# A decoder layer on one core: wide and narrow products in runs, a start with products of zeros, x loaded in quarters, and two token tiles on one weight unit

## The chip, the cores and the metric

The kernel runs on one core of one Trainium2 chip. The metric is the device time of one execution in microseconds. The kernel before took 653.57 us, the median of three runs (653.36 to 656.71).

## The reference

One post-norm decoder layer on x of 256 tokens by 1024 channels, in float32: a half-step SwiGLU, then attention and a gated short convolution side by side, then a second half-step SwiGLU, each with a residual and a layer norm.

```python
def swiglu(x, w_up, w_down):
    gate, up = jnp.split(x @ w_up, 2, axis=-1)
    return (jax.nn.silu(gate) * up) @ w_down

def hybrid_mixer(x, w_in, b_gate, conv_w, conv_b, w_proj_attn, w_proj_conv, w_out):
    z = x @ w_in                                  # q, k, v, h, g_b, g_c, gates
    y_attn = moba_attention(heads(q), heads(k), heads(v)) @ w_proj_attn
    y_conv = (g_b * short_conv(g_c * h, conv_w, conv_b)) @ w_proj_conv
    gate_attn, gate_conv = jnp.split(jax.nn.sigmoid(gates + b_gate), 2, axis=-1)
    return (gate_attn * y_attn + gate_conv * y_conv) @ w_out

x = layer_norm(ALPHA * x + 0.5 * swiglu(x, ffn1_w_up, ffn1_w_down), ln1_g, ln1_b)
x = layer_norm(ALPHA * x + hybrid_mixer(x, ...), ln2_g, ln2_b)
x = layer_norm(ALPHA * x + 0.5 * swiglu(x, ffn2_w_up, ffn2_w_down), ln3_g, ln3_b)
```

w_up is 1024 x 5632, w_down 2816 x 1024, w_in 1024 x 8192, and the three square matrices are 1024 x 1024. With 256 tokens there is one attention block, so attention is plain causal attention over 8 heads.

## The kernel before, in words

**Numbers in two parts.** Products run on float32r operands. Every operand a is split into a high part hi (a cast on ScalarE) and a low part lo = a - hi (a subtraction on VectorE), and a product is made of three passes: hi by hi, hi by lo, lo by hi. `split` (L175) does it for activations, `prep` (L809) for weights.

**Units.** The weights come in units of 128 x 2048 numbers (1 MB). SyncE loads a unit into one of three buffers `raw` (`load`, L799, the DMA at L804), ScalarE writes its high part (L814) and VectorE its low part (L817) into two of ten buffers `S`, in 2 chunks, or in 4 for the first two units of the layer. Such a buffer set is then used by TensorE until its last product.

**Three kinds of products.** `rows` (L268): the activations of one tile of 128 tokens are the stationary operand (the weights in the array), 512 columns of the unit move past them; 24 products of 512 columns for one tile and 512 outputs, over two units. `cols` (L290): 128 columns of the unit are stationary, the activations of both tiles move. For each of 8 slices k of the contraction there are two products. The wide one has u.hi stationary and 512 moving columns (the high parts of 256 tokens, then their low parts); the narrow one has u.lo stationary and 256 columns (high parts alone). The 16 products of such a group accumulate in one PSUM bank; `both` (L314) adds the two halves of the bank. `D` in `ffn` (L372): hidden activations stationary, w_down moving, 512 columns (256 at the very end).

In `cols` wide and narrow come in turns, but for the last slice, where the narrow one goes first:

```python
            two = [mm(... u.hi ..., k == 0, k == KT - 1, 512, u),
                   mm(... u.lo ..., False, False, 256, u)]
            ops += two if k < KT - 1 else two[::-1]
```

**Order.** The program is one list of products, `base`, written in the order of the layer. Transposes and attention are inserted at offsets in microseconds of a model clock (`put`, L112; L774 to L785). A last loop (L852) emits the list; before each product `advance` (L829) issues loads and casts ahead, as far as buffers and some constants allow. All engines then run their own instructions in that order and wait for each other by semaphores.

**The start.** SyncE loads tile 0 of x in two halves (`load_x(0)`, L446), the first unit in four quarters, tile 1 of x (L806), the second unit in four quarters. TensorE transposes x through PSUM, 128 columns at a time, four to a bank (`XT`, L245), and ScalarE and VectorE split the result into the tile `X`. Then `U_rows(0, 0)` and `U_rows(0, 1)` take the first 256 gate and 256 up columns of w_up by `rows`: all 24 products of tile 0 over both units, then all 24 of tile 1, with tile 1's transposes inserted. `U_cols` (L349) follows for the other hidden columns. Line numbers with L are those of the profile.

Of the kernel before, what the change touches and what calls it, by code (L numbers as in the profile page):

```python
# [9 lines left out]
F = mybir.dt.float32  # L10
R = mybir.dt.float32r
# [12 lines left out]
SCALE = 128 ** -0.5  # L24
NEG = -3.0e38

LEAD, LEAD0, LEAD1, PACE, DELAY, QUIET = 30.0, 0.1, 0.9, 2.2, 1.2, 4.0
OFF, AT0, AT1, AT2, HEAD = 5.0, 1.3, 10.5, 15.0, 7.5
AD1, AD2, AD3 = 2.0, 1.5, 1.0
S_BUFS, X_BUFS, RAW_BUFS, N_BUFS, T_BUFS, ACC_BUFS = 10, 3, 3, 9, 8, 8  # L30
# [35 lines left out]
def layer(ctx: ExitStack, tc: tile.TileContext, a: dict, out: bass.AP):  # L66
# [14 lines left out]
    state = {"dma": 0, "prep": 0, "chunk": 0, "t": -100.0, "hold": 0, "quiet": 0.0}  # L81


    ident = sb.tile([128, 128], F, name="ident")
    make_identity(nc, ident)
    mask = sb.tile([128, 128], F, name="mask")
# [3 lines left out]
    mhalf = sb.tile([128, 1], F, name="mhalf")  # L90
    nc.gpsimd.memset(mhalf, -0.5)
    cvec = sb.tile([128, 48], F, name="cvec")
    warm = sb.tile([128, 1], F, name="warm")
    nc.scalar.activation(warm, mhalf, AF.Silu)

# [4 lines left out]
    def mm(dst, lhsT, rhs, start, stop, cols, unit=None):  # L100
        return Op(lambda: nc.tensor.matmul(dst(), lhsT=lhsT(), rhs=rhs(), start=start, stop=stop), cols, unit)  # L101
# [10 lines left out]
    def put(at, dt, ops):  # L112

        ins.append((at, dt, ops))
# [6 lines left out]
    def new_unit(src, chunks=2):  # L121
        u = Unit(src, chunks)
        units.append(u)
        return u

    def row_units(w, c0, chunks=2, gap=None):

        res = []
        for kh in range(2):
            rows = w[kh * 512:(kh + 1) * 512, :]  # L130

            def src(raw, rows=rows):
# [24 lines left out]
    def transposes(src, n, evac):  # L157

        box = {}

        def go(i):
            if i == 0:
                box["t"] = ACC.get()
            nc.tensor.transpose(box["t"][:, i * 128:(i + 1) * 128], src(i), ident)  # L164

        ops = [Op(lambda i=i: go(i), 256) for i in range(n)]

        def fin():
            evac(box["t"])
            ACC.free()  # L170

        ops[-1].after.append(fin)
        return ops
# [94 lines left out]
    def rows(key, t, uns, epi):  # L268

        box, ops = {}, []  # L270
        for k in range(KT):
            u = uns[k // 4]
            ops += passes(lambda: box["b"], lambda s, k=k: st["xT", key][:, k, s, t, :],
                          lambda w, u=u, k=k: (u.hi, u.lo)[w][:, (k % 4) * 512:(k % 4 + 1) * 512],
                          k == 0, k == KT - 1, 512, u)
        f0 = ops[0].fn

        def first():
            box["b"] = ACC.get()
            f0()  # L280

        def fin():
            epi(box["b"])
            ACC.free()

        ops[0].fn = first
        ops[-1].after.append(fin)
        return add(ops)

    def cols(key, u, b, epi):  # L290

        box, ops = {}, []
        for k in range(KT):
            c = slice(k * 256 + b * 128, k * 256 + (b + 1) * 128)
            two = [mm(lambda: box["b"], lambda c=c: u.hi[:, c],
                      lambda k=k: st["xT", key][:, k].rearrange("p s t n -> p (s t n)"), k == 0, k == KT - 1, 512, u),
                   mm(lambda: box["b"][:, 0:256], lambda c=c: u.lo[:, c],
                      lambda k=k: st["xT", key][:, k, 0].rearrange("p t n -> p (t n)"), False, False, 256, u)]
            ops += two if k < KT - 1 else two[::-1]
        f0 = ops[0].fn  # L300

        def first():
            box["b"] = ACC.get()
            f0()

        def fin():
            epi(box["b"])
            ACC.free()

        ops[0].fn = first  # L310
        ops[-1].after.append(fin)
        return add(ops)
# [6 lines left out]
    def ffn(key, wu, wd, ln_i, by_rows, order, tail, after_ln):  # L319
# [9 lines left out]
        def U_rows(j, t):  # L329
            if j not in wun:  # L330
                wun[j] = row_units(wu, j * 256, 4 if key == "x" else 2, DFF)

            def epi(bank):
                sc = T.get()
                nc.scalar.activation(sc[:, 0:256], bank[:, 0:256], AF.Silu)
                nc.vector.tensor_tensor(sc[:, 256:512], sc[:, 0:256], bank[:, 256:512], op=OP.mult)
                st["h", j, t] = sc

            end = rows(key, t, wun[j], epi)
# [7 lines left out]
            put(end, OFF, transposes(lambda i: st["h", j, t][:, 256 + i * 128:256 + (i + 1) * 128], 2, evac))  # L347

        def U_cols(j):  # L349
            ug, uu = col_unit(wu, j * 256), col_unit(wu, DFF + j * 256)  # L350
# [63 lines left out]
                    op.after.insert(0, lambda: T.free(2))  # L414
            return add(ops)

        for j, t in order:
            U_rows(j, t)
        js = [j for j in range(by_rows, NJ)]
        done = 0  # L420
        for j in js:
# [12 lines left out]
        return e0, e1  # L434


    x2 = a["x"][0]
    for t in range(2):
        st["x", t] = N.get()

    def load_x(t):
        for h in range(2):
            c = slice(h * 512, (h + 1) * 512)
            nc.sync.dma_start(st["x", t][:, c], x2[t * 128:(t + 1) * 128, c])  # L444

    load_x(0)  # L446
    crow = sb.tile([48, 128], F, name="crow")

    def load_vectors():
# [4 lines left out]
    for half in range(2):  # L454
        add(XT("x", 0, lambda: st["x", 0], half))
    for half in range(2):
        put(len(base), 3.9 + 0.9 * half, XT("x", 1, lambda: st["x", 1], half))

    e0, e1 = ffn("x", a["ffn1_w_up"][0], a["ffn1_w_down"][0], 1, 1, ((0, 0), (0, 1)), 3, lambda t: ln_fin(t, 1))
    gb1_at = e0 - 150  # L460
    xt_after("m", 0, e0, 6.0, 6.9)
    xt_after("m", 1, e1, 8.2, 9.1)
# [336 lines left out]
    def load():  # L799
        while state["dma"] < len(order) and RAW.live < RAW_BUFS:  # L800
            u = order[state["dma"]]
            u.raw = RAW.get()
            for view, src in u.src(u.raw):
                nc.sync.dma_start(view, src)  # L804
            if state["dma"] == 0:
                load_x(1)  # L806
            state["dma"] += 1

    def prep(u, c):  # L809
# [77 lines left out]
```

## Time and profile before

| | |
|---|---|
| median of 3 runs | 653.57 us (653.36 to 656.71) |
| the profiled execution | 653.16 us, span of its instructions 651.3 us |
| TensorE products (PE) | 638.8 us busy, 98% of the span |
| weight loads into the array (PEld) | 547.5 us, 84% |
| VectorE (DVE), ScalarE (ACT), GpSimd (POOL) | 450.1 us, 357.1 us, 17.8 us |
| DMA | 121.18 MB, mean 186 GB/s |

How to read it: busy time of PE counts every product from its start to its modelled end, and products overlap, so neighbouring busy times add up to more than the span. The distance from one start to the next is what a product costs in a stream. A row of the timeline or of the chain merges products that follow each other with the same tiles, of whatever shape (the shape printed is one of them); its start is exact, so the difference of two rows' starts is the time of everything between. Idle time of the other engines costs nothing while TensorE goes on.

### The profile page before, as it was taken

The page shows a single profiled execution, that of the slowest core. Times are in us where ns is not written, and L with a number is a line of the kernel's source. Part 1 is how long each engine was busy: PE and PEld are TensorE (multiplying, and loading weights), DVE is VectorE, ACT ScalarE, POOL GpSimd, SP SyncE. Part 2 cuts the span into 40 slices and gives each one's busy share as a digit, 9 for nine tenths or more (in the row PEclk, how much of TensorE's full clock was granted, in tenths as well). Part 3 has the DMA queues.
Part 4 walks back from the last instruction along what each step waited for, and adds up shares of the span by engine and source line. Part 5 has one row for each costly group of instructions (what it writes and reads, how often), then busy time and mean ns, then how long its engine had stood idle before and what let it go on. Part 6 is the DMA issues. An engine that isn't in the chain of part 4 may idle for free.

```text
span 651.3 us, 8759 instructions
## 1 busy us (share of the span) xinstructions
PE 638.8 (98%) x3431; PEld 547.5 (84%) x3431; DVE 450.1 (69%) x707; ACT 357.1 (55%) x608; POOL 17.8 (3%) x26
## 2 busy tenths in 40 slices
PE   7999999999999999999999999999999999999995
PEld 5888888888888888888888888888888888888884
DVE  4786666666678576778659987886866666666636
ACT  4775555555534557667578655551556555555510
POOL 2000000000011000000000000001100000000002
PEclk9999999999999999999999999999999999999998
DMA  8856666557645572546647755572556755555301
GB/s 286 295 196 219 210 217 210 185 191 250 201 130 156 168 227 96 172 152 193 196 129 210 243 194 194 194 227 97 192 193 199 257 194 195 194 193 194 130 1 65
DMA packets 95853, 121.18 MB, mean 186 GB/s; under 512 B 2196, under 2 KB 84420, under 8 KB 95812
## 3 DMA queue, kind: packets, MB, share of 16 engines
q1 hardware_dynamic: 95812, 120.62, 56.9%
q8 instruction: 27, 0.44, 0.3%
q14 instruction: 14, 0.11, 0.0%
HBM read 119.56 MB, written 1.05 MB: 185 GB/s over the span
## 4 chain that ended last, share of the span: by engine, by line
PE 97%; DMA 1%; SPq 1%; POOL 0%; DVE 0%; issue 0%; ACT 0%; POOLq 0%
PE acc L101 96%; PE acc L164 1%; DMA raw<-in_ffn_w_up 1%; SPq L804 0%; SPq L444 0%; POOL rs L224 0%; POOL nmr L751 0%; DVE S L817 0%; ACT S L814 0%; POOLq L883 0%; POOL N L754 0%; DVE bn L214 0%; DVE N L212 0%; DVE mv L220 0%; PE acc L646 0%
## 5 line engine op out<-in xcount | busy, mean ns | idle before, releaser
L101 PE MATMUL acc<-X,S 128*128 128x512 f32 (+1 forms) x2368 | 424.5, 340 | 0.0
L101 PEld LDWEIGHTS acc<-X,S 128*128 128x128 f32 x2368 | 363.8, 189 | 53.5
L817 DVE TENSOR_TENSOR S<-raw,S 128x1024 fp32r<-128x1024 f32 (+1 forms) x224 | 268.5, 1205 | 43.4 <-ACT S L814 41.9
L814 ACT CAST S<-raw 128x1024 fp32r<-128x1024 f32 (+1 forms) x224 | 228.3, 1035 | 54.7 <-PE acc L101 49.3
L101 PE MATMUL acc<-S,T 128*128 128x512 f32 (+1 forms) x546 | 123.5, 383 | 0.0
L101 PEld LDWEIGHTS acc<-S,T 128*128 128x128 f32 x546 | 100.1, 188 | 19.4
L316 DVE TENSOR_TENSOR T<-T,acc 128x256 f32<-128x256 f32 x124 | 52.1, 420 | 86.4 <-ACT T L315 86.3
L315 ACT COPY T<-acc 128x256 f32<-128x256 f32 x124 | 46.1, 372 | 109.2 <-PE acc L101 108.2
L101 PE MATMUL acc<-S,X 128*128 128x512 f32 x336 | 82.8, 403 | 1.1 <-ACT S L814 0.9
L101 PEld LDWEIGHTS acc<-S,X 128*128 128x128 f32 x336 | 63.6, 193 | 16.0 <-ACT S L814 1.7
L177 ACT CAST X<-acc 128x512 fp32r<-128x512 f32 (+1 forms) x24 | 12.4, 516 | 27.5 <-PE acc L164 14.8
L187 ACT CAST T<-T 128x256 fp32r<-128x256 f32 x38 | 15.5, 408 | 19.3 <-DVE T L361 19.3
L178 DVE TENSOR_TENSOR X<-acc,X 128x512 fp32r<-128x512 f32 (+1 forms) x24 | 14.3, 598 | 14.7 <-ACT X L177 14.6
L355 ACT ACTIVATE T<-T 128x256 f32<-128x256 f32 x38 | 15.9, 418 | 11.2 <-DVE T L316 11.1
L212 DVE SCALAR_TENSOR_TENSOR N<-acc,N 128x512 f32<-128x512 f32 (+1 forms) x13 | 8.4, 644 | 15.8 <-PE acc L101 15.8
L224 POOL TENSOR_TENSOR rs<-ve,mhalf 128x1 f32<-128x1 f32 x6 | 5.8, 964 | 466.1 <-DVE ve L222 466.1
L182 DVE TENSOR_TENSOR T<-T,T 128x256 fp32r<-128x256 f32 x38 | 16.0, 420 | 1.9 <-ACT T L187 1.9
L361 DVE TENSOR_TENSOR T<-T 128x256 f32<-128x256 f32 x38 | 16.2, 425 | 1.3
L316 DVE TENSOR_TENSOR N<-N,acc 128x256 f32<-128x256 f32 x24 | 10.0, 418 | 9.1 <-ACT N L315 9.1
L315 ACT COPY N<-acc 128x256 f32<-128x256 f32 x24 | 8.9, 370 | 12.6 <-PE acc L101 12.3
L182 DVE TENSOR_TENSOR S<-T,S 128x256 fp32r<-128x256 f32 x16 | 6.8, 422 | 9.6 <-ACT S L187 9.6
L178 DVE TENSOR_TENSOR T<-acc,T 128x128 fp32r<-128x128 f32 (+1 forms) x20 | 7.9, 395 | 5.4 <-ACT T L177 5.4
(68 smaller groups left out, 199.7 us busy)
## 6 DMA issues: line engine op xcount, KB each, us to landing
raw<-in_ffn_w_up SPq DMA_DIRECT2D x38, 1024.0 KB, 5.1
raw<-in_w_in SPq DMA_DIRECT2D x32, 1024.0 KB, 5.5
raw<-in_ffn_w_down SPq DMA_DIRECT2D x22, 1024.0 KB, 4.9
raw<-in_w_proj_attn SPq DMA_DIRECT2D x4, 1024.0 KB, 5.1
raw<-in_w_proj_conv SPq DMA_DIRECT2D x4, 1024.0 KB, 5.0
raw<-in_w_out SPq DMA_DIRECT2D x4, 1024.0 KB, 4.9
raw<-in_ffn_w_up SPq DMA_DIRECT2D x8, 512.0 KB, 5.0
raw<-in_ffn_w_up SPq DMA_DIRECT2D x8, 256.0 KB, 5.8
```

Source lines behind the costliest of these rows:

```text
L101: return Op(lambda: nc.tensor.matmul(dst(), lhsT=lhsT(), rhs=rhs(), start=start, stop=stop), cols, unit)
L177: nc.scalar.copy(hi, src)
L178: nc.vector.tensor_tensor(lo, src, hi.bitcast(F), op=OP.subtract)
L182: nc.vector.tensor_tensor(lo, src, hi.bitcast(F), op=OP.subtract)
L187: nc.scalar.copy(hi, src)
L212: nc.vector.scalar_tensor_tensor(y[:, c], src, scale, st["ax", t][:, c], op0=OP.mult, op1=OP.add)
L315: nc.scalar.copy(dst, bank[:, 256:512])
L316: nc.vector.tensor_tensor(dst, dst, bank[:, 0:256], op=OP.add)
L355: defer(0.8, lambda: nc.scalar.activation(g[:, 0:256], g[:, 0:256], AF.Silu))
L361: nc.vector.tensor_tensor(g[:, 0:256], g[:, 0:256], g[:, 256:512], op=OP.mult)
L814: nc.scalar.copy(u.hi[:, s], u.raw[:, s])
L817: nc.vector.tensor_tensor(u.lo[:, s], u.raw[:, s], u.hi[:, s].bitcast(F), op=OP.subtract)
```

## The change

1. `cols` issues its sixteen products in runs: the first seven wide ones, the eight narrow ones, the last wide one.
2. The first two units are used by both tiles at once (`rows_both`, new): for each unit, the 12 products of tile 0 and then the 12 of tile 1, each tile in its own PSUM bank. Transposes of x stand between them.
3. x is loaded in four quarters of 128 x 512. The first goes out on ScalarE's queue ahead of its table load; the other three stand on SyncE's queue, one after the first two quarters of the first unit and two after its last (`early`).
4. Before the first transposes TensorE makes six products of 512 columns from a tile of zeros, `still`, which GpSimd fills first of all, and three more after the first four transposes (`idle`, new). Nothing reads their results.
5. The constant LEAD0 goes from 0.1 to -1.0, which delays the casts of weights in the list at the very start.

```diff
-LEAD, LEAD0, LEAD1, PACE, DELAY, QUIET = 30.0, 0.1, 0.9, 2.2, 1.2, 4.0
+LEAD, LEAD0, LEAD1, PACE, DELAY, QUIET = 30.0, -1.0, 0.9, 2.2, 1.2, 4.0
...
+    still = T.get(R)
+    nc.gpsimd.memset(still.bitcast(F), 0.0)
     ident = sb.tile([128, 128], F, name="ident")
...
+    load_x(0, 0, nc.scalar)
     warm = sb.tile([128, 1], F, name="warm")
     nc.scalar.activation(warm, mhalf, AF.Silu)
...
+    def idle(n):
+
+        def go():
+            b = ACC.get()
+            for i in range(n):
+                nc.tensor.matmul(b, lhsT=still[:, 0:128], rhs=still, start=i == 0, stop=i == n - 1)
+            ACC.free()
+
+        return [Op(go, 512 * n)]
...
+    def rows_both(key, uns, epis, between):
...
+        for half in range(2):
+            for t in range(2):
+                for k in range(half * 4, half * 4 + 4):
+                    u = uns[half]
+                    ops += passes(lambda t=t: box[t], lambda s, k=k, t=t: st["xT", key][:, k, s, t, :],
+                                  lambda w, u=u, k=k: (u.hi, u.lo)[w][:, (k % 4) * 512:(k % 4 + 1) * 512],
+                                  k == 0, k == KT - 1, 512, u)
...
+        for i in range(len(ops)):
+            for extra in between.get(i, []):
+                add(extra)
+            add([ops[i]])
...
     def cols(key, u, b, epi):
-        box, ops = {}, []
+        box, wide, narrow = {}, [], []
         for k in range(KT):
...
-            ops += two if k < KT - 1 else two[::-1]
+            wide.append(mm(lambda: box["b"], lambda c=c: u.hi[:, c],
...
+            narrow.append(mm(lambda: box["b"][:, 0:256], lambda c=c: u.lo[:, c],
...
+        ops = wide[:-1] + narrow + wide[-1:]
...
-        for j, t in order:
-            U_rows(j, t)
+        if key == "x":
+            U_both(0, order)
+        else:
+            for j, t in order:
+                U_rows(j, t)
...
-    load_x(0)
+    early = {1: [(1, 0)], 3: [(0, 1), (1, 1)]}
...
+    add(idle(6))
+    add(xts[0, 0])
+    add(idle(3))
+    base[-1].after.append(T.free)
+    e0, e1 = ffn("x", a["ffn1_w_up"][0], a["ffn1_w_down"][0], 1, 1,
+                 {6: [xts[1, 0]], 12: [xts[0, 1]], 18: [xts[1, 1]]}, 3, lambda t: ln_fin(t, 1))
...
-            for view, src in u.src(u.raw):
+            for i, (view, src) in enumerate(u.src(u.raw)):
                 nc.sync.dma_start(view, src)
-            if state["dma"] == 0:
-                load_x(1)
+                for t, h in early.get(i, []) if state["dma"] == 0 else []:
+                    load_x(t, h, nc.sync)
```

**On TensorE, one column group.** Before, the first group of `U_cols`; X are the activations, S_172 the unit's high part, S_173 its low part:

```order
L101 MATMUL acc_235<-X_102,S_172 128x512
L101 MATMUL acc_235<-X_102,S_173 128x256
L101 MATMUL acc_235<-X_102,S_172 128x512
L101 MATMUL acc_235<-X_102,S_173 128x256
L101 MATMUL acc_235<-X_102,S_172 128x512
L101 MATMUL acc_235<-X_102,S_173 128x256 x2
L101 MATMUL acc_235<-X_102,S_172 128x512
```

The same place in the changed kernel and the group behind it (S_195 and S_196 are the two parts, T_213 the hidden activations of tile 0):

```order
L112 MATMUL acc_163<-S_150,X_111 128x512
L112 MATMUL acc_235<-X_111,S_195 128x512 x7
L112 MATMUL acc_235<-X_111,S_196 128x256 x8
L185 MATMUL acc_255<-ident,T_213 128x128 x2
L112 MATMUL acc_235<-X_111,S_195 128x512
L112 MATMUL acc_271<-X_111,S_195 128x512 x7
L112 MATMUL acc_271<-X_111,S_196 128x256 x8
L112 MATMUL acc_271<-X_111,S_195 128x512
```

The last wide product of a group and the seven of the next stand in a row, so switches between the two widths go from fifteen a group to two. The transposes of tile 0's hidden activations, which before stood ahead of the first group, now stand inside it.

**On TensorE, the start.** The changed kernel's first rows (T_63 is the tile of zeros, N_78 and N_79 tiles 0 and 1 of x, S_118 and S_119 the first unit's two parts):

```order
L142 MATMUL acc_99<-T_63 128x512 x6
L185 MATMUL acc_106<-ident,N_78 128x128 x4
L142 MATMUL acc_114<-T_63 128x512 x3
L112 MATMUL acc_128<-S_118,X_111 128x512
L112 MATMUL acc_128<-S_119,X_111 128x512
L112 MATMUL acc_128<-S_118,X_111 128x512 x2
L112 MATMUL acc_128<-S_119,X_111 128x512
L112 MATMUL acc_128<-S_118,X_111 128x512
L185 MATMUL acc_137<-ident,N_79 128x128 x4
```

Before, the first rows were eight transposes of N_78, and then all 24 products of tile 0 over both units.

**On SyncE, the first loads.** Before (raw_83 and raw_90 are the first two units, raw_95 the third):

```order
L444 DMA N_78<-in_x 128x512 x2
L804 DMA raw_83<-in_ffn_w_up 128x2x256 x4
L444 DMA N_79<-in_x 128x512 x2
L804 DMA raw_90<-in_ffn_w_up 128x2x256 x4
L804 DMA raw_95<-in_ffn_w_up 128x8x256
```

In the changed kernel (raw_84, raw_92 and raw_97 in their places):

```order
L860 DMA raw_84<-in_ffn_w_up 128x2x256 x2
L101 DMA N_79<-in_x 128x512
L860 DMA raw_84<-in_ffn_w_up 128x2x256 x2
L101 DMA N_78<-in_x 128x512
L101 DMA N_79<-in_x 128x512
L860 DMA raw_92<-in_ffn_w_up 128x2x256 x4
L860 DMA raw_97<-in_ffn_w_up 128x8x256
```

Two quarters of weights now lead SyncE's queue, where two of x did; the quarter of x that is needed first is on ScalarE's queue.

## Rows read from the trace of the kernel before

**Rows 1.** The page: busy time of TensorE, and the chain that ended last, by engine.

```profile
PE 638.8 (98%) x3431; PEld 547.5 (84%) x3431; DVE 450.1 (69%) x707; ACT 357.1 (55%) x608; POOL 17.8 (3%) x26
...
PE 97%; DMA 1%; SPq 1%; POOL 0%; DVE 0%; issue 0%; ACT 0%; POOLq 0%
```

**Rows 2.** TensorE's two longest waits over the whole span: us in total, times, longest.

```profile
PE acc L164 <- DMA N<-in_x: 3.6, 1, 3.6
PE acc L101 <- ACT S L814: 0.9, 1, 0.9
```

**Rows 3.** Groups by line and shape, whole span: count, busy us, mean ns of one, idle.

```profile
L101 PE MATMUL acc<-X,S 128*128 128x512 f32 x1184 | 411.0, 398 | 0.0
...
L101 PE MATMUL acc<-X,S 128*128 128x256 f32 x1184 | 308.8, 281 | 0.0
...
L101 PEld LDWEIGHTS acc<-S,T 128*128 128x128 f32 x546 | 100.1, 188 | 19.4
...
L101 PE MATMUL acc<-S,T 128*128 128x256 f32 x36 | 4.5, 283 | 0.0
```

**Rows 4.** Timeline of TensorE, two stretches: start us, length us, what, count.

```profile
44.80 5.62 PE L101 MATMUL acc<-S,T 128*128 128x512 f32 x24
50.26 11.44 PE L101 MATMUL acc<-X,S 128*128 128x512 f32 x64
61.54 5.61 PE L101 MATMUL acc<-S,T 128*128 128x512 f32 x24
66.98 1.22 PE L101 MATMUL acc<-X,S 128*128 128x512 f32 x6
...
639.03 4.47 PE L101 MATMUL acc<-S,T 128*128 128x256 f32 x36
```

**Rows 5.** The chain that ended last, in order of time, from 475 us.

```profile
476.00 5.46 PE acc L101 x24
481.46 0.22 PE acc L164 x2
481.68 5.64 PE acc L101 x32
```

**Rows 6.** Timeline of the first 23 us, all engines, and of TensorE alone there.

```profile
0.27 0.10 POOL L876 MEMSET const-float32-1.0<- 128x1 f32 x1
...
0.71 0.21 POOL masks.py:197 MEMSET ident<- 128x128 f32 x1 [0.29 <-POOLq L876]
...
3.56 1.94 PE L164 MATMUL acc<-ident,N 128*128 128x128 f32 x8 [3.56 <-DMA N<-in_x]
...
4.68 0.59 ACT L177 CAST X<-acc 128x512 fp32r<-128x512 f32 x1 [2.47 <-PE acc L164]
...
6.35 0.69 DVE L817 TENSOR_TENSOR S<-raw,S 128x512 fp32r<-128x512 f32 x1 [0.36 <-ACT S L814]
...
6.37 6.03 PE L101 MATMUL acc<-S,X 128*128 128x512 f32 x13 [0.87 <-ACT S L814]
...
11.22 2.88 ACT L814 CAST S<-raw 128x512 fp32r<-128x512 f32 x4 [1.54 <-DMA raw<-in_ffn_w_up]
...
16.50 1.05 ACT L814 CAST S<-raw 128x1024 fp32r<-128x1024 f32 x1 [1.09 <-DMA raw<-in_ffn_w_up]
...
17.58 1.23 DVE L817 TENSOR_TENSOR S<-raw,S 128x1024 fp32r<-128x1024 f32 x1 [1.46 <-ACT S L814]
...
22.02 5.85 PE L101 MATMUL acc<-X,S 128*128 128x512 f32 x32
...
7.69 4.04 PE L101 MATMUL acc<-S,X 128*128 128x512 f32 x9
...
11.53 0.87 PE L101 MATMUL acc<-S,X 128*128 128x512 f32 x2
12.62 1.72 PE L101 MATMUL acc<-S,X 128*128 128x512 f32 x6 [0.22 <-DVE S L817]
```

**Rows 7.** Busy us of each engine in the first stretch, granted clock, DMA share, GB/s.

```profile
0.00:11.90 11.90, 7.47 (x20) 5.29 (x21) 3.90 (x7) 5.45 (x9) 3.28 (x11) 1.00 0.82 262
```

More of the change, by code (lines that the diff above doesn't have):

```diff
@@ L92, in layer, with load_x @@
     cvec = sb.tile([128, 48], F, name="cvec")
+    x2 = a["x"][0]
+    for t in range(2):
+        st["x", t] = N.get()
+    def load_x(t, h, engine):
+        c = slice(h * 512, (h + 1) * 512)
+        engine.dma_start(st["x", t][:, c], x2[t * 128:(t + 1) * 128, c])
+    load_x(0, 0, nc.scalar)
     warm = sb.tile([128, 1], F, name="warm")
@@ L288, in rows, with first, fin @@
         return add(ops)
+    def rows_both(key, uns, epis, between):
+        box, ops = {}, []
+        for half in range(2):
+            for t in range(2):
+                for k in range(half * 4, half * 4 + 4):
[3 more added lines that the diff above has]
+                                  k == 0, k == KT - 1, 512, u)
+        for t in range(2):
+            def first(t=t, f0=ops[12 * t].fn):
+                box[t] = ACC.get()
+                f0()
+            def fin(t=t):
+                epis[t](box[t])
+                ACC.free()
+            ops[12 * t].fn = first
+            ops[12 * t + 35].after.append(fin)
+        for i in range(len(ops)):
+            for extra in between.get(i, []):
+                add(extra)
+            add([ops[i]])
+        return len(base)
     def cols(key, u, b, epi):
-        box, ops = {}, []
+        box, wide, narrow = {}, [], []
         for k in range(KT):
             c = slice(k * 256 + b * 128, k * 256 + (b + 1) * 128)
[L295 to L298, printed above, removed]
-            ops += two if k < KT - 1 else two[::-1]
+            wide.append(mm(lambda: box["b"], lambda c=c: u.hi[:, c],
+                           lambda k=k: st["xT", key][:, k].rearrange("p s t n -> p (s t n)"),
+                           k == 0, k == KT - 1, 512, u))
+            narrow.append(mm(lambda: box["b"][:, 0:256], lambda c=c: u.lo[:, c],
+                             lambda k=k: st["xT", key][:, k, 0].rearrange("p t n -> p (t n)"), False, False, 256, u))
+        ops = wide[:-1] + narrow + wide[-1:]
         f0 = ops[0].fn
@@ L327, in hT_of, with U_epi, hT_put @@
             return st["hT", key, j, kk]
[L329 to L339, printed above, removed]
+        def U_epi(j, t, bank):
+            sc = T.get()
+            nc.scalar.activation(sc[:, 0:256], bank[:, 0:256], AF.Silu)
+            nc.vector.tensor_tensor(sc[:, 256:512], sc[:, 0:256], bank[:, 256:512], op=OP.mult)
+            st["h", j, t] = sc
+        def hT_put(j, t, at, dt):
             def evac(bank):
@@ L345, in evac, with U_rows, U_both @@
                     split(hT[:, 0], hT[:, 1], bank[:, kk * 128:(kk + 1) * 128])
-            put(end, OFF, transposes(lambda i: st["h", j, t][:, 256 + i * 128:256 + (i + 1) * 128], 2, evac))
+            put(at, dt, transposes(lambda i: st["h", j, t][:, 256 + i * 128:256 + (i + 1) * 128], 2, evac))
+        def U_rows(j, t):
+            if j not in wun:
+                wun[j] = row_units(wu, j * 256, 2, DFF)
+            hT_put(j, t, rows(key, t, wun[j], lambda bank: U_epi(j, t, bank)), OFF)
+        def U_both(j, between):
+            end = rows_both(key, row_units(wu, j * 256, 4, DFF),
+                            [lambda bank, t=t: U_epi(j, t, bank) for t in range(2)], between)
+            for t in range(2):
+                hT_put(j, t, end, OFF - 2.7 * (1 - t))
         def U_cols(j):
@@ L452, in load_vectors @@
         nc.sync.dma_start(crow[32:48], a["b_gate"][0].rearrange("(c p) -> c p", p=128))
[L454 to L459, printed above, removed]
+    xts = {(t, half): XT("x", t, lambda t=t: st["x", t], half) for t in range(2) for half in range(2)}
+    add(idle(6))
[4 more added lines that the diff above has]
+                 {6: [xts[1, 0]], 12: [xts[0, 1]], 18: [xts[1, 1]]}, 3, lambda t: ln_fin(t, 1))
     gb1_at = e0 - 150
```

7 lines of the change are left out of this document (removed).

## Prediction

> **What bounds the kernel now.** I read four views, in this order. The page's busy table and its chain of waits come first: TensorE is busy for 638.8 of 651.3 us, and 97% of the chain that ended last is products of TensorE [rows 1]. The reader should then ask whether TensorE ever waits. The list of TensorE's waits answers it: two waits of note, 4.5 us in all, and what they wait for (x, the first cast) belongs to the start [rows 2]. No transfer, no cast and no VectorE work holds TensorE up after that. What is left is what TensorE's own products cost one after another, and the first 22 us.
>
> The third view is the grouping of TensorE's work by shape: 1184 products of 512 columns (wide) and 1184 of 256 columns (narrow) come from the column helper, in 148 groups of 8 and 8 [rows 3]. A product's busy time there (398 and 281 ns) says little, because products overlap. What counts is the distance from one start to the next, so the fourth view is the timeline of TensorE, where the starts of neighbouring merged rows give the sums.
>
> - Wide in a run: 24 wide products take 50.26 - 44.80 = 5.46 us, and 66.98 - 61.54 = 5.44 us; 227 ns each [rows 4].
> - Wide and narrow in turns: 64 products, four column groups, take 61.54 - 50.26 = 11.28 us, which is 2.82 us a group [rows 4]. The chain gives the same in another place: 5.64 us for two groups, beside 5.46 us for 24 wide ones [rows 5].
> - Narrow in a run: 36 of them stretch over 4.47 us, of which the last one's own 283 ns is a tail: (4.47 - 0.28) / 35 = 120 ns each [rows 3, 4].
>
> So eight wide and eight narrow products would take 8 x 0.227 + 8 x 0.120 = 2.776 us if each kind ran as it does in runs, and they take 2.82 us in turns.
>
> **Runs in place of turns.** The change issues seven wide, eight narrow and one wide product; since the next group begins with wide ones, TensorE sees eight of a kind in a row. No instruction is added, and no operand differs. The gain is 2.820 - 2.776 = 44 ns a group, less what the two switches cost. A switch is not shown by itself; the nearest rows are the two stretches of 24 wide products, both entered from a column group: 5.46 and 5.44 us. One switch therefore costs 0.02 us more than another at most. I take 2 ns of it, near the cheap end, because the 120 ns of the narrow run already contain its entry. That makes 42 ns x 148 = **6.2 us**. The ends: with a full 0.02 us at the switch 24 ns x 148 = 3.6 us, and with 8 x 0.2267 (the 5.44 us) and 8 x 0.1197 and no price for a switch 48 ns x 148 = 7.1 us. All of it lies on the path, as TensorE waits for nothing there. The order also moves needs: the fifth wide product, which is the first to need the second half of a unit's high part, comes after 4 x 0.227 = 0.9 us instead of 1.4 us, and the low part is first needed after 1.6 us instead of 0.2 us. Casts that now precede TensorE without any wait cover a shift of half a microsecond.
>
> **The first 22 us.** Before, the first wide product starts at 6.37 us, and the next nine starts run from 7.69 to 11.53 us, 427 ns apart: that is 512 columns at 1.2 GHz. [...] (The column for the granted clock reads 1.00 for these first microseconds too [rows 7], which the distances contradict, so I read the level from the distances.) The 13 products from 6.37 to 12.62 us take 6.25 us instead of 13 x 0.227 = 2.95 us: 3.3 us are there to be had. The first column group starts at 22.02 us.
>
> The products of zeros give TensorE work earlier. The zeros come from a fill on GpSimd of 512 columns. Fills of 1 and of 128 columns take 0.10 and 0.21 us [rows 6], so some 0.5 us, from 0.7 to 1.25 us. Six products at 427 ns last from 1.3 to 3.9 us; x's quarter, issued at once on ScalarE's queue, should be there as before (3.56 us), so waiting for the zeros costs the first transpose 0.3 us. The cast of the transposes begins 1.12 us after the first of them (4.68 against 3.56), so at 5.0; 0.59 us for it and 0.62 us for the first quarter of weights give a first real product at about 6.3 us, **as before**. Nothing is won by an earlier start; what can be won is the clock. Before, it rose between 11.5 and 12.6 us, 5.2 to 6.2 us after the first wide product. From 1.3 us the same delay gives 6.5 to 7.5 us; I take 7.
>
> From there casts set the pace of the first quarters: VectorE's parts at 0.69 us each end near 6.95, 7.6, 8.3 and 9.0 us, so the tile's first 12 products end at about 9.9 us, the transposes woven between them included. Then, all at the higher clock: two sets of four transposes at 0.44 us, 12 products of the other tile, 24 products of the second unit, (12 + 24) x 0.227 + 0.88 = 9.05 us. The first column group starts at 18.95 us: 3.05 us earlier. One pair of transposes, 0.22 us [rows 5], which stood ahead of 22.02 us, now comes later. Net **2.8 us**. Are the weights there? ScalarE casts the four quarters of the second unit from 11.22 us on, waiting for the first; the last product needs the last one near 15.7 us, and they may only come earlier, as SyncE now issues weights first and passes one quarter of x to ScalarE's queue. The third unit is cast from 16.50 us, when it has landed: its halves are ready at 17.6 and 18.6 us, needed from 18.95 and 19.9 us; its low parts follow at 1.23 us a half, by 20.0 us, needed from 20.55 us. That fits, with half a microsecond to spare in the tightest place. The ends: if the clock rises no earlier than before, nothing is won; if the casts did not bind, 48 x 0.227 + 1.3 us from 6.3 us end at 18.5 us, which gives 3.3 us.
>
> Two tiles on a unit at once, seen alone, cost and save nothing in products. They halve the rate at which the first two units are wanted, which is why the higher clock can be used in spite of transfers. The ScalarE issue of 0.4 us stands before a table load that nobody waits for.
>
> **Sum.** 653.16 - 6.2 - 2.8 = 644.2 us against the profiled execution. That execution lies 0.4 us under the median of the three runs shown (653.57), so I forecast **644.6 us**. A measurement of this kernel can tell about 0.5%, some 3.3 us, from no change.
>
> **Rivals.**
> 1. The runs pay, the head does not: products of zeros leave the clock where it was, or transfers arrive so that 22.0 us stands. For it: no row here shows TensorE on zeros, and ScalarE waited 1.5 us for weights at 11.22 us. Against: the nine slow products were back to back, so it was the clock and not the data that bound them. 653.6 - 6.2 - 0.2 = 647.2 us.
> 2. The neighbours do not matter: a product's price depends on its columns alone, and the 2.82 us stay. Speaking for it: the runs of the trace take other weights and another moving operand than the column helper does. Against: both runs of wide products, with weights from different tiles, agree within 2 ns: those of [rows 4] hold hidden activations as weights, the 24 at 476.00 us of [rows 5] the layer's own. Then the head alone: 653.6 - 2.8 = 650.8 us. [...]
> 3. Slower: eight narrow products in a row run into their weight loads. A load takes 188 ns [rows 3], more than a narrow product; in turns every second product is wide and covers it. If loads cannot overlap each other, a narrow product in a run costs 188 ns, 8 x 68 ns x 148 = 81 us more: about 732 us. It decides as soon as a narrow product's distance passes 125 ns. Against it stand the 36 narrow products at 120 ns, each with a load of its own.
> 4. The change does not do what it says on the chip: wide and narrow stay mixed by a wait, for the second half of a unit, say. The orders above exclude it as far as the program goes; it would end near rival 2's time.
>
> **How the numbers follow.** Forecast 0.75; rival 1 0.13; rivals 2 and 4 0.09; rival 3 0.03. The forecast's own range is 653.6 less 3.6 to 7.1 and 0 to 3.3 us: 643.2 to 650, most of it below 647. Reaching up to rival 1, and down for a faster switch than I priced, 642.6 to 647.8 us leaves out the last 0.12 and the thin ends. Faster by over 0.5% (below 650.3): forecast and rival 1 with their ends, 0.88. Within: rivals 2 and 4, 0.09. Slower: rival 3, 0.03.
>
> **What would show it.** In the profile after, 64 products of column groups should take 11.1 us; more than 11.25 us proves the second step wrong. The first wide product of the layer should start near 6.3 us, the fifth and later at 227 ns once casts allow, and the first column group at about 19 us. If wide products still stand 427 ns apart at 9 us, the zeros failed. TensorE's waits should stay inside the first 10 us; a wait on a cast near 19 us would mean that the third unit came late.

## The result and the profile after

The changed kernel takes 649.80 us, the median of four runs (649.58 to 650.08), where the kernel before takes 653.47 us in the same comparison: a ratio of 0.9942, with a 95% interval of 0.9928 to 0.9957. It is faster by 0.6%, as the sign of the forecast said, but by 3.7 us and not by 9: 649.8 lies above the range of 642.6 to 647.8 us. The profiled execution took 650.08 us with a span of 648.1 us (before: 653.16 and 651.3), so the two traces differ by 3.2 us.

The page's busy line after the change, beside [rows 1]:

```profile
PE 638.3 (98%) x3440; PEld 548.9 (85%) x3440; DVE 449.8 (69%) x707; ACT 354.2 (55%) x608; POOL 18.5 (3%) x27
```

The list of TensorE's waits over the whole span, beside [rows 2] (us in total, times, longest):

```profile
PE acc L142 <- POOL T L85: 1.3, 1, 1.3
PE acc L112 <- ACT S L870: 0.3, 1, 0.3
PE acc L112 <- DVE S L873: 0.3, 1, 0.3
```

TensorE is still all of the kernel. The longest wait is now the one for the zeros, until 1.29 us, and behind the start there is none. So whatever is missing from the forecast sits in the starts of the products, not in a wait. First the head, in the timeline of TensorE (start us, length us, what, count, idle time before it):

```profile
1.29 2.93 PE L142 MATMUL acc<-T 128*128 128x512 f32 x6 [1.29 <-POOL T L85]
4.02 1.05 PE L185 MATMUL acc<-ident,N 128*128 128x128 f32 x4
4.73 1.21 PE L142 MATMUL acc<-T 128*128 128x512 f32 x3
6.27 0.50 PE L112 MATMUL acc<-S,X 128*128 128x512 f32 x1 [0.34 <-ACT S L870]
7.08 1.43 PE L112 MATMUL acc<-S,X 128*128 128x512 f32 x5 [0.31 <-DVE S L873]
8.35 0.60 PE L185 MATMUL acc<-ident,N 128*128 128x128 f32 x4
8.70 1.90 PE L112 MATMUL acc<-S,X 128*128 128x512 f32 x6
10.44 0.60 PE L185 MATMUL acc<-ident,N 128*128 128x128 f32 x4
...
12.61 7.08 PE L112 MATMUL acc<-S,X 128*128 128x512 f32 x30
19.53 2.70 PE L112 MATMUL acc<-X,S 128*128 128x512 f32 x15
```

The first real product starts at 6.27 us (before 6.37), and the first column group at 19.53 us instead of 22.02 [rows 6]. One pair of transposes, 0.22 us, now comes behind that point, so the head gained 2.3 us.

Then the stretch that answers to [rows 4], in the same columns:

```profile
42.29 5.75 PE L112 MATMUL acc<-S,T 128*128 128x512 f32 x24
47.88 11.31 PE L112 MATMUL acc<-X,S 128*128 128x512 f32 x64
59.03 5.75 PE L112 MATMUL acc<-S,T 128*128 128x512 f32 x24
64.62 5.73 PE L112 MATMUL acc<-X,S 128*128 128x512 f32 x32
```

Two things moved here, in opposite directions. Four column groups take 59.03 - 47.88 = 11.15 us instead of 11.28. Over all groups with nothing woven in, the mean of their starts went from 2.822 us (132 groups) to 2.794 us (131): 28 ns x 148 = 4.1 us gained. (By the order shown ahead of the prediction, a group before changes width fourteen times, not the fifteen named there; now it does so twice.) But the 24 wide products between the groups, those of `D`, take 47.88 - 42.29 = 5.59 us instead of 5.46 and 5.44: **233 ns each instead of 227**. The grouping by shape, first of the kernel before and then of the changed one, has the loss for the whole group (count, busy us, mean ns of one, idle):

```profile
L101 PE MATMUL acc<-S,T 128*128 128x512 f32 x510 | 119.2, 390 | 0.0
...
L112 PE MATMUL acc<-S,T 128*128 128x512 f32 x510 | 122.2, 395 | 0.0
```

There are 510 products, and their busy time is 3.0 us more than before. Taken from the starts, 5.8 ns x 510 = 3.0 us lost; over all neighbours within `D` the mean distance is 227.3 ns before and 233.3 ns after. The sum is -2.3 - 4.1 + 3.0 = -3.4 us, against -3.2 us of the spans.

Nothing in the change names `D`. The study therefore asked what made those 510 products dearer, and then what each of the two gains was made of.

### The profile page after: what moved, and what is told of

Same layout as the page of the kernel before. It is cut to its first block, busy times and chain, and to the rows that moved or that the text cites. A ratio compares the mean times of both kernels' runs of the same rounds, so it can differ in the third digit from the quotient of the medians.

```text
span 648.1 us, 8783 instructions
## 1 busy us (share of the span) xinstructions
PE 638.3 (98%) x3440; PEld 548.9 (85%) x3440; DVE 449.8 (69%) x707; ACT 354.2 (55%) x608; POOL 18.5 (3%) x27
## 4 chain that ended last, share of the span: by engine, by line
PE 98%; POOL 0%; DVE 0%; issue 0%; ACT 0%; POOLq 0%; DVEq 0%
PE acc L112 96%; PE acc L185 1%; PE acc L142 0%; POOL rs L245 0%; POOL nmr L807 0%; DVE S L873 0%; ACT X L198 0%; POOL T L85 0%; POOLq L939 0%; POOL N L810 0%; DVE bn L235 0%; DVE N L233 0%; DVE mv L241 0%; PE acc L702 0%; DVE ve L243 0%
## 5 line engine op out<-in xcount | busy, mean ns | idle before, releaser
L112 PE MATMUL acc<-S,T 128*128 128x512 f32 (+1 forms) x546 | 126.4, 387 | 0.0
L112 PE MATMUL acc<-S,X 128*128 128x512 f32 x336 | 80.3, 394 | 0.7 <-ACT S L870 0.3
L112 PEld LDWEIGHTS acc<-S,X 128*128 128x128 f32 x336 | 62.1, 188 | 14.2 <-DVE S L873 1.1
L416 ACT ACTIVATE T<-T 128x256 f32<-128x256 f32 x38 | 15.9, 418 | 11.6 <-DVE T L371 11.6
L198 ACT CAST T<-acc 128x128 fp32r<-128x128 f32 (+1 forms) x20 | 7.0, 350 | 7.8 <-DVE T L199 4.0
```

The costliest lines, as they stand in the source:

```text
L198: nc.scalar.copy(hi, src)
L416: defer(0.8, lambda: nc.scalar.activation(g[:, 0:256], g[:, 0:256], AF.Silu))
```

## The experiments

All of them compute the full layer. Each is compared with the kernel before, whose median lies between 653.3 and 653.6 us in all comparisons. Two theories for `D` stood at the start: the **place** of a buffer in SBUF (the tile of zeros is the first thing that pool T is asked for; pools are laid out in the order of first use, so T moves from byte 211104 of each partition, the top, to byte 16512, and raw, X and S move up by 16384; these places are worked out from the order and the sizes of the buffers in the kernels, as a trace shows no addresses), and the **entry** (a run of `D` now begins behind seven or eight narrow ones and a wide one).

**1. The runs alone.** The kernel before with the new order in `cols` and nothing else.

```diff
-            ops += two if k < KT - 1 else two[::-1]
...
+            wide.append(mm(... u.hi ..., 512, u))
+            narrow.append(mm(... u.lo ..., 256, u))
+        ops = wide[:-1] + narrow + wide[-1:]
```

> The kernel before with the new order of the column groups alone; T stays at the top of SBUF. Seen so far: in the changed kernel the products with hidden activations as weights (weights from T) stand 233 ns apart instead of 227, 510 of them, 3.1 us. Theory A (place): the tile of zeros is the first that asks for pool T, so T moves from the top of SBUF to its bottom, and loading weights from there slows the products. Then here they stay at 227 ns, the column groups take 2.793 us, and the time is 653.5 - 148 x 0.027 = 649.5 us. Theory B (entry): a run of wide products keeps the rhythm in which it is entered, and one wide product behind eight narrow ones starts the slow rhythm. Then they stand at 233 ns here too, and the time is 652.6 us.

Measured 649.62 us, ratio 0.9941 (0.9926 to 0.9956). TensorE's timeline:

```profile
44.62 5.62 PE L101 MATMUL acc<-S,T 128*128 128x512 f32 x24
50.08 11.31 PE L101 MATMUL acc<-X,S 128*128 128x512 f32 x64
```

`D` stays at 5.46 us for 24. The runs alone bring 4.0 us, no less than the whole change with its head: the order of the groups is not what hurt `D`.

**2. The place alone.** The kernel before, with pool T asked for first and given back at once. Not one instruction changes, only addresses.

```diff
+    T.get(R)
+    T.free()
     ident = sb.tile([128, 128], F, name="ident")
```

> The kernel before, in which nothing is changed but that one buffer of pool T is asked for and given back before any other tile, so that T lies at the bottom of SBUF as in the changed kernel. Theory A (place): products with weights from T at 233 ns, 653.5 + 3.1 = 656.6 us. Theory B (entry): 227 ns and 653.5 us.

Measured 656.00 us, ratio 1.0039 (1.0025 to 1.0054). TensorE's timeline:

```profile
44.61 5.75 PE L103 MATMUL acc<-S,T 128*128 128x512 f32 x24
50.20 11.43 PE L103 MATMUL acc<-X,S 128*128 128x512 f32 x64
61.47 5.75 PE L103 MATMUL acc<-S,T 128*128 128x512 f32 x24
```

50.20 - 44.61 = 5.59 us for 24, as in the changed kernel, while four column groups in turns take 11.27 us, as before. The place alone costs 2.4 us in medians, where theory A had 3.1 (the spans of the two traces, 653.9 and 651.3 us, lie 2.6 us apart).

**3. The change with the old places.** The zeros come from a buffer of pool N, whose place doesn't depend on it.

```diff
-    still = T.get(R)
+    still = N.get(R)[:, 0:512]
...
-    base[-1].after.append(T.free)
+    base[-1].after.append(N.free)
```

> The changed kernel with its zeros in a buffer of pool N instead of T, so that T, S, X and raw lie where they lay before. Theory A (place): products with weights from T at 227 ns, 649.8 - 3.1 = 646.7 us. Theory B (entry): 233 ns and 649.8 us.

Measured 647.43 us, ratio 0.9909 (0.9892 to 0.9925), 2.4 us below the change, where theory A had 3.1. TensorE's timeline:

```profile
42.09 5.62 PE L112 MATMUL acc<-S,T 128*128 128x512 f32 x24
47.55 11.32 PE L112 MATMUL acc<-X,S 128*128 128x512 f32 x64
58.70 5.62 PE L112 MATMUL acc<-S,T 128*128 128x512 f32 x24
```

`D` is back at 5.46 us, and the 64 products keep their 11.15 us. The following kernels start from this one where nothing else is said.

**4. The narrow run elsewhere.** The changed kernel, with one wide product ahead of the narrow run and seven behind it, so that `D` follows a run of wide ones.

```diff
-        ops = wide[:-1] + narrow + wide[-1:]
+        ops = wide[:1] + narrow + wide[1:]
```

> The changed kernel (T at the bottom) with the eight narrow products behind the first wide one, so that the last seven wide ones of a group lead into the products with weights from T. Theory A (place): these stay at 233 ns, the time stays within 0.3 us of 649.8. Theory B (entry): the run is in its fast rhythm when they come, 227 ns and 646.7 us. Under both a column group should stay near 2.793 us.

Measured 650.52 us, ratio 0.9955 (0.9940 to 0.9970). In its timeline `D` still takes 5.60 us:

```profile
42.30 5.75 PE L112 MATMUL acc<-S,T 128*128 128x512 f32 x24
47.90 11.34 PE L112 MATMUL acc<-X,S 128*128 128x512 f32 x64
59.08 5.75 PE L112 MATMUL acc<-S,T 128*128 128x512 f32 x24
```

The entry theory falls a second time. The median is 0.7 us above the change, and not within 0.3 us as theory A had it; the column groups take 59.08 - 47.90 = 11.18 us for four instead of 11.15, and why is open.

**5. No products of zeros.** Kernel 3 without its nine `idle` products, to see what they are worth; their buffer is given back at once.

```diff
-    add(idle(6))
     add(xts[0, 0])
-    add(idle(3))
...
+    N.free()
```

> As e3_old_places (647.4 us), without the nine products of zeros. Theory C (clock): the zeros are what raises TensorE's clock early; without them the wide products stand 427 ns apart until some 5.5 us after the first one, near 11.8 us, some 12 of them at 0.2 us more each, 2.4 us, and the time is 649.8 us, about that of e1_runs_only: quarters of x and both tiles on one unit bring nothing by themselves. Theory D (data): the order of loads and of tiles brings the gain; the time stays within 0.5 us of 647.4.

Measured 649.11 us, ratio 0.9934 (0.9917 to 0.9950): between the two theories, nearer to the clock's. TensorE's timeline:

```profile
3.53 1.08 PE L185 MATMUL acc<-ident,N 128*128 128x128 f32 x4 [3.53 <-DMA N<-in_x]
5.80 3.31 PE L112 MATMUL acc<-S,X 128*128 128x512 f32 x6 [1.19 <-ACT S L868]
8.91 1.06 PE L185 MATMUL acc<-ident,N 128*128 128x128 f32 x4
9.62 2.91 PE L112 MATMUL acc<-S,X 128*128 128x512 f32 x6
12.32 0.64 PE L185 MATMUL acc<-ident,N 128*128 128x128 f32 x4
12.72 1.66 PE L112 MATMUL acc<-S,X 128*128 128x512 f32 x6
14.21 0.60 PE L185 MATMUL acc<-ident,N 128*128 128x128 f32 x4
...
21.50 1.75 PE L112 MATMUL acc<-X,S 128*128 128x512 f32 x7
```

and of kernel 3, which has the zeros, at the same places:

```profile
4.73 1.63 PE L142 MATMUL acc<-N 128*128 128x512 f32 x3
6.27 2.27 PE L112 MATMUL acc<-S,X 128*128 128x512 f32 x6
8.38 0.60 PE L185 MATMUL acc<-ident,N 128*128 128x128 f32 x4
8.73 1.64 PE L112 MATMUL acc<-S,X 128*128 128x512 f32 x6
10.20 0.60 PE L185 MATMUL acc<-ident,N 128*128 128x128 f32 x4
10.56 1.64 PE L112 MATMUL acc<-S,X 128*128 128x512 f32 x6
12.04 0.60 PE L185 MATMUL acc<-ident,N 128*128 128x128 f32 x4
...
19.30 2.70 PE L112 MATMUL acc<-X,S 128*128 128x512 f32 x15
```

Without zeros the first product comes half a microsecond sooner, at 5.80 us, but the first three sets of six products take 8.91 - 5.80 = 3.11 us, 12.32 - 9.62 = 2.70 us and 14.21 - 12.72 = 1.49 us, where kernel 3 takes 2.11, 1.47 and 1.48 us. Six at the 427 ns of [rows 6] are 2.56 us, six at 227 ns 1.36 us: the long distances last until about 12.3 us here. The first column group starts at 21.50 us, with zeros at 19.30 us. The zeros are thus worth 2.2 us in starts and 1.7 us in medians. The rest of the start, 22.02 - 21.50 less 0.22 us of transposes, is 0.3 us. Quarters of x, two tiles on one unit and the new LEAD0 share it; no run separates them.

**6 and 7. What about the place?** Kernel 3 with T elsewhere. In 6 raw, X and T are asked for in that order behind the first small tiles, so that T lies below S, at byte 129184, and S at 145568, as in the change. In 7 T is asked for before raw, so that raw, X and S lie exactly as in the change, and T at 55456 below them all.

```diff
     crow = sb.tile([48, 128], F, name="crow")
+    for pool in (RAW, X, T):
+        pool.get()
+        pool.free()
```

```diff
     crow = sb.tile([48, 128], F, name="crow")
+    T.get()
+    T.free()
```

> As e3_old_places, with pool T between X and S (byte 129184 of a partition), which moves S up by 16384 bytes, to where the changed kernel has it; raw and X stay. Theory A1 (T at the bottom is what costs): weights from T at 227 ns, 647.4 us. Theory A2 (the new place of S, which moves past those weights, is what costs): 233 ns, 650.5 us.

> As e3_old_places, with pool T between N and raw (byte 55456): raw, X and S lie as in the changed kernel, T and N have changed places with each other. Theory A1: if any place far below S costs, 233 ns and 650.5 us; if only the lowest bytes do, 227 ns and 647.4 us. Theory A2 (place of S): 233 ns and 650.5 us. With e6 the three tell apart: 227 and 227 ns leaves the lowest bytes alone, 227 and 233 ns the distance below S, 233 and 233 ns the place of S.

Both measured 647.26 us, ratio 0.9908 (0.9894 to 0.9923 and 0.9893 to 0.9923), and both have `D` at 5.47 and 5.46 us. The timeline of 7:

```profile
42.05 5.62 PE L112 MATMUL acc<-S,T 128*128 128x512 f32 x24
47.51 11.32 PE L112 MATMUL acc<-X,S 128*128 128x512 f32 x64
```

Neither the place of S, nor T below S, nor a distance between them costs anything. Of the changed kernel's layout two things are left: that T is the lowest pool, and the exact byte. The buffers of X, S and T, and the slices of them that products take, lie at multiples of 512 bytes from their pool's start, so the pool's start counts. In the kernel before, in 3, 6 and 7, T and S both start 160 bytes past a multiple of 512. In the change and in 2, T starts at 128 and S at 160.

**8. Two groups woven.** Kernel 3 with both column groups of a unit at once: 14 wide, 16 narrow, 2 wide. It has half the switches.

```diff
-        ops = wide[:-1] + narrow + wide[-1:]
...
+        return add(wide[0][:-1] + wide[1][:-1] + narrow[0] + narrow[1] + wide[0][-1:] + wide[1][-1:])
```

> As e3_old_places, with the two column groups of a unit woven: sixteen wide products, then sixteen narrow ones, so half as many switches. In e3 a wide run needs five products behind a switch to come down to 227 ns (234, 235, 229, 232, 231), 26 ns in all over 5 x 227. If that is a price of the switch, a pair of groups takes 5.56 us instead of 5.587, 74 x 26 ns = 1.9 us less: 645.5 us. If the epilogues of two groups that now come together hold TensorE up, more than 647.4 us, with waits on ScalarE or VectorE.

Measured 646.35 us, ratio 0.9895 (0.9880 to 0.9910). TensorE's timeline:

```profile
47.59 11.28 PE L112 MATMUL acc<-X,S 128*128 128x512 f32 x64
58.71 5.61 PE L112 MATMUL acc<-S,T 128*128 128x512 f32 x24
```

It is the fastest kernel of the study, 1.1 us below kernel 3 where 1.9 were expected. The 64 products went from 11.15 to 11.12 us: half the switches gone are worth 8 ns a group here, 1.1 us over 148 of them. TensorE waits for nothing behind the start in this trace either.

**9. Byte 160 for T, low in SBUF.** The changed kernel with 32 bytes before and behind T: T at 160 past a multiple of 512, S at 224.

```diff
+    sb.tile([128, 8], F, name="pad0")
     still = T.get(R)
+    sb.tile([128, 8], F, name="pad1")
```

> The changed kernel with T still the lowest pool, but 32 bytes higher (16544 in place of 16512) and everything above it 64 bytes higher. In all kernels with 227 ns S, X and T began 32 bytes past a multiple of 64; with 233 ns T began at a multiple of 64 and S did not. Theory A4 (the lowest bytes): T is still there, 233 ns, 649.8 us. Theory A5 (alignment): T, X and S are all 32 past a multiple of 64 again, 227 ns and 647.3 us.

Measured 648.64 us, ratio 0.9930 (0.9914 to 0.9947): neither theory. `D` takes 47.55 - 42.04 = 5.51 us for 24, 229.6 ns each, by this timeline:

```profile
42.04 5.67 PE L114 MATMUL acc<-S,T 128*128 128x512 f32 x24
47.55 11.33 PE L114 MATMUL acc<-X,S 128*128 128x512 f32 x64
```

The edit moved S and X as well as T, so it made T and S differ by 64 bytes instead of 32. That pointed to the difference between the two starts.

**10. T off by 32 at the top.** Kernel 3 with 32 bytes between S and T: T at 192 past a multiple of 512, S at 160.

```diff
+    for pool in (RAW, X, S):
+        pool.get()
+        pool.free()
+    sb.tile([128, 8], F, name="pad0")
+    T.get()
+    T.free()
```

> As e3_old_places (T at the top, 647.4 us), with 32 unused bytes between S and T, so that T alone begins at a multiple of 64 (211136). Theory A4 (the lowest bytes): 227 ns, 647.4 us. Theory A5 (alignment): 233 ns for weights from T, 649.9 us.

Measured 650.23 us, ratio 0.9953 (0.9938 to 0.9968). TensorE's timeline:

```profile
41.89 5.75 PE L112 MATMUL acc<-S,T 128*128 128x512 f32 x24
47.49 11.34 PE L112 MATMUL acc<-X,S 128*128 128x512 f32 x64
```

32 bytes at the top of SBUF cost as much as the move to the bottom did: 5.60 us for 24. So T need not be the lowest pool for the loss. Whether the lowest place adds anything of its own was not run: no kernel has T there with the start of S.

**11. All pools off by 32.** Kernel 3 with 32 bytes below raw: raw, X, S and T all start at 192.

```diff
     crow = sb.tile([48, 128], F, name="crow")
+    sb.tile([128, 8], F, name="pad0")
```

> As e3_old_places, with 32 unused bytes below raw, so that raw, X, S and T all begin at a multiple of 64. Theory A4: no change, 647.4 us. Theory A5 in the form that weights at a multiple of 64 are slow whatever moves past them: every wide product in a run goes to 233 ns, those of the column groups and of the layer's rows too, some 1900 at up to 6 ns, up to 11 us more, 658 us. Theory A5 in the form that weights and moving operand must lie alike: 227 ns everywhere, 647.4 us.

Measured 647.23 us, ratio 0.9909 (0.9894 to 0.9924). TensorE's timeline:

```profile
42.03 5.62 PE L112 MATMUL acc<-S,T 128*128 128x512 f32 x24
47.49 11.31 PE L112 MATMUL acc<-X,S 128*128 128x512 f32 x64
```

`D` takes 5.46 us. It is not one good byte that counts, but that both operands start alike.

**12. T off by 64.** Kernel 10 with 64 bytes in place of 32: T at 224, S at 160.

```diff
-    sb.tile([128, 8], F, name="pad0")
+    sb.tile([128, 16], F, name="pad0")
```

> As e3_old_places, with 64 unused bytes between S and T. Seen so far for weights from T with S moving past them: T and S the same distance past a multiple of 128 give 227 ns (four kernels at three places), 32 apart 233 ns (at the bottom and at the top), 64 apart and T at the bottom 229.6 ns. Theory E (only the difference of the two counts): 229.6 ns here too, some 500 x 2.2 ns = 1.1 us more than e3, 648.5 us. Theory F (the 229.6 ns are what the lowest place costs by itself): 227 ns and 647.4 us.

Measured 650.05 us, ratio 0.9947 (0.9930 to 0.9964). TensorE's timeline:

```profile
41.84 5.76 PE L112 MATMUL acc<-S,T 128*128 128x512 f32 x24
47.43 11.32 PE L112 MATMUL acc<-X,S 128*128 128x512 f32 x64
```

`D` takes 5.59 us. It fits neither expectation: kernel 9, with T 64 bytes less than S, had 229.6 ns, and this one, with T 64 bytes more, has 233. A period of 128 bytes in the difference alone, as the expectations have it, cannot tell these two apart, so it is not the whole rule. The two kernels also differ in the place of T (bottom and top) and in the starts of S and X, and no run separates that from the sign.

**13. X off by 32.** Kernel 3 with 32 bytes between X and S: S and T at 192, X at 160. If the rule is one of operands, it must hold for products that have nothing to do with T.

```diff
     crow = sb.tile([48, 128], F, name="crow")
+    for pool in (RAW, X):
+        pool.get()
+        pool.free()
+    sb.tile([128, 8], F, name="pad0")
```

> As e3_old_places, with 32 unused bytes between X and S: S and T lie alike, X lies 32 off both. Theory E, if it holds for every product: weights from T keep 227 ns; the 336 products with the layer's activations as weights go to 233 ns, 1.9 us; the wide products of the column groups, 230.8 ns in the mean, lose their fast rhythm, 1184 x 3 ns = 3.5 us: about 652.8 us. If the difference matters only to weights from T: 647.4 us.

Measured 651.78 us, ratio 0.9974 (0.9962 to 0.9986), 4.4 us above kernel 3, where 5.4 were expected. TensorE's timeline in two places:

```profile
42.28 5.60 PE L112 MATMUL acc<-S,T 128*128 128x512 f32 x24
47.72 11.42 PE L112 MATMUL acc<-X,S 128*128 128x512 f32 x64
58.98 5.60 PE L112 MATMUL acc<-S,T 128*128 128x512 f32 x24
...
474.17 5.85 PE L112 MATMUL acc<-S,X 128*128 128x512 f32 x24
479.86 0.38 PE L185 MATMUL acc<-ident,T 128*128 128x128 f32 x2
```

and the changed kernel at the place of the last two rows:

```profile
472.20 5.74 PE L112 MATMUL acc<-S,X 128*128 128x512 f32 x24
477.78 0.38 PE L185 MATMUL acc<-ident,T 128*128 128x128 f32 x2
```

`D`, whose operands lie alike, takes 5.44 us for 24. The column groups rise to 58.98 - 47.72 = 11.26 us for four, where kernel 3 has 11.15, and 24 products with X as weights from 477.78 - 472.20 = 5.58 to 479.86 - 474.17 = 5.69 us. The tax has moved from T's products to X's. The groupings by shape of kernel 3 and of this one have it for all 336 products with X as weights (count, busy us, mean ns of one, idle):

```profile
L112 PE MATMUL acc<-S,X 128*128 128x512 f32 x336 | 80.4, 394 | 0.0
...
L112 PE MATMUL acc<-S,X 128*128 128x512 f32 x336 | 81.8, 398 | 0.8 <-ACT S L874 0.5 <-DVE S L877 0.3
```

## Why the prediction was wrong, point by point

**"No instruction is added, and no operand differs" is the step that failed.** The sum put every product that the change does not name at no change, and gave no reason for it but this sentence. Its first half holds for `cols`, and the operands of `D` hold the same numbers, but in other bytes: asking T for the zeros before anything else moved the pool. That term was missing, with +3.0 us by the starts. Run 2 has it alone (+2.4 us in medians), run 3 has the change without it, and its 647.43 us would have been inside the range, near its upper end, because the next term came short too. The edit that did it looks like a detail of the zeros. It should have been asked of every new request to a pool what else it moves.

**The runs were mis-sized.** Their mechanism was right: 64 products took 11.15 us, under the bound of 11.25, and run 1 shows 4.0 us from the order alone. The term was 6.2 us, and 4.1 came. The price of a switch was what I chose worst: 2 ns of the 20 that my rows allowed. The starts of single products in a run that follows narrow ones show it: in the changed kernel, from 50.42 us on, they stand 233, 236, 228, 233, 230 ns apart, then 227. Entering that wide run costs 25 ns, spread over five products. The narrow ones are entered at 113 ns (49.58 us), 7 ns less than the 120 ns that I took, which leaves some 18 ns for the two switches of a group. The stretches of 24 that I compared were entered from column groups, and in the kernel before the one at 44.80 us opens late as well (235, 229, 232, 231 ns, then 227); so both held the price, and their agreement said nothing of its size. By the gain itself, 44 - 28 = 16 ns a group were missing; halving the switches (run 8) gave back 8 of them. The lower end of that term, 3.6 us, was sound.

**The head was right but for half a microsecond.** Predicted were 2.8 us net, and 2.3 came. The first real product started at 6.27 us (I had 6.3). The distances fell near the 7 us that I took, or sooner: in the six products at the start they are 427 ns, but the last two of the three that follow stand 236 ns apart, before 6 us. In the trace of kernel 3 those three stretch over 1.63 us instead of 1.21, and its products take 2.11 us for six from 6.27 us on and 1.47 us from 8.73 us on. Run 5 shows that it is the zeros that bring this forward. That a clock stands behind the distances was my estimate: the 1.2 GHz that I named is 512 columns over 427 ns, in the kernel before single starts stand 229 and 235 ns apart from 12.96 us on, no view shows a frequency, and the granted clock reads 1.00 in the first 12 us of the change too. What came later than planned were the weights. The timeline of ScalarE and VectorE at the third quarter of the first unit:

```profile
7.79 1.30 ACT L870 CAST S<-raw 128x512 fp32r<-128x512 f32 x2 [1.06 <-DMA raw<-in_ffn_w_up]
...
8.45 1.37 DVE L873 TENSOR_TENSOR S<-raw,S 128x512 fp32r<-128x512 f32 x2 [0.82 <-ACT S L870]
```

ScalarE waited 1.06 us for that quarter's DMA, so the low part of the third quarter ended near 9.1 us and not at 8.3. The chain that ended last passes that point on TensorE, which goes on at 9.20 us. The first tile's twelve products were done by 10.44 us, and I had 9.9. The loads, not only the casts, set the pace there. Of the half microsecond 0.2 us is not firm: kernel 3, with the same head, starts its first column group at 19.30 us. The third unit was in time, as said: no wait near 19 us.

**Rivals.** Rival 1 named 647.2 us, and run 3 came out at 647.4, but by other terms: the zeros did work there. Rival 2 falls with run 1. Rival 3, narrow products slowed by their weight loads, falls too: groups became cheaper. Rival 4 falls with the 11.15 us. What happened was no rival of mine: a loss in products that the change does not name.

## What to carry to other kernels

A kernel that is one long stream of products, each with a new set of weights, can pay for the bytes at which its operands start: here up to 6 ns of 227 for each. Where weights and moving operand come from different pools, let both begin at the same number of bytes past a multiple of 512, as in runs 3, 6, 7 and 11 (227 ns), and look at the layout again whenever an edit adds a tile or asks a pool earlier. After any change, compare the distances of products in the groups that were not touched; here they held back 2.4 of the 6.2 us that run 3 has. And a price that two rows share cannot be read from their difference: it needs a row that doesn't have it.

## What the runs showed of the hardware

**Where operands start.** A product of 512 columns with a new set of weights follows the one before by 227 ns when its weights and its moving operand start alike (three places of T, two values of the start: runs 3, 6, 7, 11), by 233 ns when the weights start 32 bytes before or behind (the change and run 2; run 10), and by 229.6 or 233 ns with 64 bytes before or behind (runs 9 and 12). Run 13 shows the same tax on other products. Slices lie at multiples of 512 bytes from their pool's start and pay nothing, so if the price repeats, its period divides 512; run 12, where T and S differ by 64 bytes and the price is paid, excludes 64. Whether it is 128, 256 or 512, whether it is the sign or the place that tells run 9 from run 12, and what makes the difference stays open.

**Entering a run of wide products has a price.** Behind the narrow products at 49.47 us of the changed kernel the next five distances of wide ones are 1 to 9 ns over 227 each, 25 ns together (233, 236, 228, 233, 230). The kernel before shows such steps too (231, 235, 229, 232, 231 ns, then 227) behind four transposes at 15.9 us. These late distances are as long as those that operands 32 bytes apart keep for the whole run (228 to 235 ns in `D` of the change at 42.29 us). In run 13, where X and S lie 32 bytes apart, `D` behind column groups of 11.26 us for four takes 5.44 us, and 5.46 us in kernel 3 behind those of 11.15 us. Whether the two prices have one cause is not shown.

**Zeros ahead bring the short distances forward.** With products whose operands are all zero ahead of the real ones, two zeros stand 236 ns apart before 6 us, after 427 ns in the first six (the change), and six real products take 1.47 us from 8.73 us on (kernel 3); without them six still take 2.70 us from 9.62 us on, and 1.49 us from 12.72 us on (run 5). Whether the clock makes the difference is not shown: its column reads 1.00 from the start in the change too.
